# One hybrid decoder step on one Trainium2 core: a convolution, three output splits and two tail norms moved to later places, gate chunks of the layer change in other banks

## The chip, the cores and the metric

The kernel runs on one core of one Trainium2 chip. The metric is the device time of one execution in microseconds (us). A core has a matrix engine (PE, with its weight load shown apart as PEld), a vector engine (DVE), a scalar engine (ACT, which also evaluates functions from tables that it loads), GpSimd (POOL) and a queue engine (SP) that issues most transfers. Matrix products land in PSUM, which is handed out here in named banks ("tr" twice, "S" once, "y" twice, "mm" three times); everything else lives in SBUF, and DRAM is reached by DMA.

## The reference

A step takes 1024 new prompt tokens and 8 sequences of 8 sample tokens (64), through two layers and a last norm, all in float32:

```python
def rmsnorm(x, g):
    xf = x.astype(jnp.float32)
    return xf * lax.rsqrt(jnp.mean(xf * xf, axis=-1, keepdims=True) + EPS) * g.astype(jnp.float32)
...
    for i in range(DEPTH):
        mod = sc @ ada_w[i].astype(jnp.float32) + ada_b[i].astype(jnp.float32)
        shift, scale, gate = jnp.split(mod, 3, axis=-1)
        hn = (rmsnorm(x, norm_g[i]) * (1.0 + scale[:, None]) + shift[:, None]).astype(x.dtype)
...
        x = (x.astype(jnp.float32) + (1.0 + gate[:, None]) * out.astype(jnp.float32)).astype(x.dtype)
    y = rmsnorm(x, final_norm_g).astype(x.dtype)
```

Layer 0 is a Mamba-2 branch: one projection gives z, x, B, C and dt; x, B and C pass a causal convolution of width 4 and a SiLU; a chunked scan over 8 groups of heads gives y; y times SiLU(z) is normed in each group and goes through an output projection. Layer 1 is a pooling branch: a projection gives u and a gate z, u is averaged over windows of 2, 4, 8 and 16 tokens, mixed inside four groups, multiplied by SiLU(z) and projected back. The outputs are y and the new states.

## The kernel before

Activations lie transposed: a tile holds 128 channels by 1088 tokens (1024 prompt, 64 sample). A product of float32 tiles is made of three matrix products of rounded parts: `split` gives hi (ACT, a copy to a rounded type) and lo (DVE, the difference), and `mm1` (lines 188 to 192) issues hi by hi, hi by lo, lo by hi; in the trace they are lines 190, 191 and 192. Weights are streamed: a DMA brings a raw tile "wr", ACT makes "wh" (line 141), DVE makes "wl" (line 145). Tokens are taken in three chunks `CH` of 368, 368 and 352 columns.

Each engine works through its own list in order. A recording layer makes the five lists: it orders the instructions of the program by itself, and `tc.issue_after(x)` puts what stands under it behind instruction x. A tile of a pool waits until the last reader of its bank or slot is done.

**The scan with projections beside it.** While the groups are scanned (`scan_group`), PE also computes the projections of later groups (`proj_group`) and then parts of the output projection. A chunk pair of a scan runs `front` (PE transposes into a "tr" bank, ACT copies Bt out of it at line 584 and makes the decay M at lines 588 and 589, DVE makes cb at line 591, M at 594 and xd at 596), `states` (PE, line 619, S from xd and Bt) and `rows` (PE into two "y" banks, lines 641 and 645, which `evac_y` adds to x on DVE, line 611). The sample tokens end a group (`back_sample`: PE line 674 into a "y" bank, then line 611 again for 64 columns; two POOL multiplications at line 678), then come the gate (`gate`: DVE line 744, ACT square line 745), the sum of the two squares (`zsum`, line 787) and the norm (line 759 and behind). A projection tile is evicted by ACT (line 436) into "raw"; with the last chunk `proj_end` runs `conv_tile`: ACT scales, DVE adds three shifted copies (line 367, 1112 columns each), ACT takes a tanh, DVE multiplies (lines 369 and 371). For the last projected group, 6, tile ii=3 is special: it runs all three chunks at once (lines 404 to 425) and its convolution is kept for later.

**Output splits.** The rows that a group leaves go to DRAM (`gyd`). For the output projection `op_part_load` fetches them in four parts of four (`op_stage`, "gr"), and `op_split` makes gh (ACT, line 800) and gl (DVE, line 801). Parts 1 and 2 are fetched and split while later groups are scanned.

**The layer change.** `ssd_out` ends layer 0. `last_part` computes the last output tiles by chunk; for each, `sq_add` squares on ACT and adds on DVE (line 859) into "ss". `done(c)` then makes the norm of chunk c (PE line 302, ACT logarithm line 305 and exponential line 318) and `modulate` gives hn as hi and lo: for each of 8 channel tiles k, DVE multiplies (line 325), ACT adds the shift in place (line 327), ACT rounds (line 328), DVE subtracts (line 329). The other form of `modulate`, used in layer 0, makes hi straight from ACT (line 331) and lo in one DVE operation (line 332). Then `plain_pairs` computes two pairs of u and gate tiles by plain products. For each chunk c two u tiles run side by side; ACT evicts them (lines 907 and 909). Behind chunk 1 stand the gate chunks 0 and 1 of tile 0, behind chunk 2 its chunk 2, then the three gate chunks of tile 1. ACT evicts a gate chunk with a SiLU (line 940). In the trace all these product tiles are "pl". Their banks come from `plain_tile(c)`: "y" for even c, "mm" for odd c. Beside this, `act_sums` (lines 994, 997 and 998) forms the sums of activations, and `w_sums` (POOL, lines 1035, 1036 and 1040) those of weights, for the fast products (lines 1070 to 1072) that follow.

**The tail.** The last output product (`pool_layer`, loops at the end) runs over two quarters c and four tiles d, 24 matrix products each ("op", lines 1289 to 1291), evicted by DVE (line 1274). The second half of the tokens was finished before, so its squares and its two quarter norms (`norm`: PE line 302, ACT lines 305, 1782 and 318; `scale`: DVE line 1795, POOL line 1793, stores from SP) stand behind the evictions of tiles d=0, 1, 2 of the first quarter:

```python
                        if d == 0:
                            square(7, HALF, HALF)
                        elif d < 3:
                            b = HALF + QUART * (d - 1)
                            p = norm(b, QUART)
```

## Time and profile before

| | |
|---|---|
| median of 3 runs | 1591.16 us (1591.13 to 1593.46) |
| the profiled execution | 1591.15 us |
| its span, first to last instruction | 1589.0 us |
| mean granted PE clock | 0.999 |
| busy: PE, PEld | 1568.2 us (99%), 1505.1 us (95%) |
| busy: DVE, ACT, POOL | 1301.7 us (82%), 790.1 us (50%), 525.5 us (33%) |
| chain that ended last: PE, DVE, DMA, ACT | 85%, 6%, 3%, 2% |

Times of single instructions are given as microseconds from the start of the span. In a row of the timeline the first two columns are start and duration, then engine, line, operation, result<-operands with their size, how many such instructions the row joins ("x4"), and in brackets how long the engine had been idle and what released it. The duration of a row counts from when the engine took the instruction, so it can hold a wait inside the engine.

### The profile page before, as it was taken

The page shows a single profiled execution, that of the slowest core. Times are in us where ns is not written, and L with a number is a line of the kernel's source. Part 1 is how long each engine was busy: PE and PEld are TensorE (multiplying, and loading weights), DVE is VectorE, ACT ScalarE, POOL GpSimd, SP SyncE. Part 2 cuts the span into 40 slices and gives each one's busy share as a digit, 9 for nine tenths or more (in the row PEclk, how much of TensorE's full clock was granted, in tenths as well). Part 3 has the DMA queues.
Part 4 walks back from the last instruction along what each step waited for, and adds up shares of the span by engine and source line. Part 5 has one row for each costly group of instructions (what it writes and reads, how often), then busy time and mean ns, then how long its engine had stood idle before and what let it go on. Part 6 is the DMA issues. An engine that isn't in the chain of part 4 may idle for free.

```text
span 1589.0 us, 30720 instructions
## 1 busy us (share of the span) xinstructions
PE 1568.2 (99%) x11946; PEld 1505.1 (95%) x11946; DVE 1301.7 (82%) x2152; ACT 790.1 (50%) x1512; POOL 525.5 (33%) x558
## 2 busy tenths in 40 slices
PE   9999999999999999999999999999999999999997
PEld 7899999999999999989999999999999999999997
DVE  6874889887899989889888858988889777667886
ACT  6663344466766666665456348433333233233373
POOL 0133456522331413141211232366666530000241
PEclk9999999999999999999999999999999999999999
DMA  9422232365555565679999432232333379565783
GB/s 356 167 101 101 80 112 84 111 194 173 161 179 165 162 209 167 212 259 297 311 332 320 164 127 69 85 121 100 117 115 115 104 250 365 140 180 178 163 172 117
DMA packets 122304, 275.57 MB, mean 173 GB/s; under 512 B 18192, under 2 KB 59312, under 8 KB 122160
## 3 DMA queue, kind: packets, MB, share of 16 engines
q1 hardware_dynamic: 118128, 260.90, 48.4%
q0 software_dynamic: 4032, 12.72, 4.7%
q8 instruction: 94, 1.54, 0.4%
q14 instruction: 50, 0.41, 0.1%
HBM read 201.12 MB, written 70.23 MB: 171 GB/s over the span
## 4 chain that ended last, share of the span: by engine, by line
PE 85%; DVE 6%; issue 3%; DMA 3%; ACT 2%; POOL 1%; SPq 0%; DVEq 0%; ACTq 0%; POOLq 0%
PE st L1070 11%; PE st L1072 11%; PE st L1071 11%; PE mm L190 10%; PE mm L191 10%; PE mm L192 10%; PE op L1289 2%; PE op L1291 2%; PE op L1290 2%; PE y L641 2%; PE S L619 2%; PE y L645 1%; PE am L261 1%; PE tr L580 1%; PE tr L577 1%
## 5 line engine op out<-in xcount | busy, mean ns | idle before, releaser
L1072 PE MATMUL st<-hh,w 128*128 128x272 f32 x832 | 240.2, 289 | 0.0
L1070 PE MATMUL st<-hh,w 128*128 128x272 f32 x832 | 240.0, 288 | 0.0
L1071 PE MATMUL st<-hl,w 128*128 128x272 f32 x832 | 240.0, 288 | 0.0
L1070 PE MATMUL st<-t,w 128*128 128x272 f32 x624 | 179.6, 288 | 0.0
L1072 PE MATMUL st<-t,w 128*128 128x272 f32 x624 | 179.5, 288 | 0.0
L1071 PE MATMUL st<-t,w 128*128 128x272 f32 x624 | 179.2, 287 | 0.0
L190 PE MATMUL mm<-hh,wh 128*128 128x368 f32 (+1 forms) x528 | 178.9, 339 | 0.0
L191 PE MATMUL mm<-hl,wh 128*128 128x368 f32 (+1 forms) x528 | 174.0, 330 | 0.0
L192 PE MATMUL mm<-hh,wl 128*128 128x368 f32 (+1 forms) x528 | 173.2, 328 | 0.0
L1070 PEld LDWEIGHTS st<-hh,w 128*128 128x128 f32 x832 | 156.7, 188 | 0.0
L1071 PEld LDWEIGHTS st<-hl,w 128*128 128x128 f32 x832 | 156.7, 188 | 0.0
L1072 PEld LDWEIGHTS st<-hh,w 128*128 128x128 f32 x832 | 156.5, 188 | 0.0
L182 ACT ACTIVATE w<-wr 128x512 fp32r<-128x512 f32 x104 | 64.9, 629 | 165.5 <-PE st L1072 134.2
L627 POOL TENSOR_TENSOR hd<-h,cd 128x256 f32<-128x256 f32 x56 | 46.1, 824 | 285.9 <-DVE h L628 135.6
L1289 PE MATMUL op<-b,w 128*128 128x272 f32 x448 | 129.4, 289 | 0.0
L1290 PE MATMUL op<-b,w 128*128 128x272 f32 x448 | 128.8, 287 | 0.2 <-DVE b L1218 0.2
L1291 PE MATMUL op<-b,w 128*128 128x272 f32 x448 | 128.9, 288 | 0.0
L190 PE MATMUL mm<-gh,wh 128*128 128x368 f32 (+1 forms) x372 | 125.3, 338 | 0.0
L192 PE MATMUL mm<-gh,wl 128*128 128x368 f32 (+1 forms) x372 | 122.4, 329 | 0.0
L191 PE MATMUL mm<-gl,wh 128*128 128x368 f32 (+1 forms) x372 | 122.2, 328 | 0.1
L1070 PEld LDWEIGHTS st<-t,w 128*128 128x128 f32 x624 | 117.6, 189 | 0.1
L1072 PEld LDWEIGHTS st<-t,w 128*128 128x128 f32 x624 | 117.3, 188 | 0.0
(310 smaller groups left out, 4596.9 us busy)
## 6 DMA issues: line engine op xcount, KB each, us to landing
wr<-win SPq DMA_DIRECT2D x48, 512.0 KB, 3.8
wr<-pin SPq DMA_DIRECT2D x32, 512.0 KB, 3.8
acb<-acd SPq DMA_DIRECT2D x60, 256.0 KB, 4.4
wr<-pout SPq DMA_DIRECT2D x28, 512.0 KB, 5.2
x<-x1d SPq DMA_DIRECT2D x24, 544.0 KB, 6.7
x1d<-x SPq DMA_DIRECT2D x22, 544.0 KB, 6.2
wr<-pout POOLq DMA_DIRECT2D x20, 512.0 KB, 6.0
x<-xT SPq DMA_DIRECT2D x16, 544.0 KB, 6.7
```

Of the source, the lines that this page charges most:

```text
L182: self.last_hi = self.nc.scalar.activation(hi, src, AF.Copy)
L190: nc.tensor.matmul(ps[:, :n], hi[:, k, :], ah[:, a:a + n], start=first, stop=False)
L191: nc.tensor.matmul(ps[:, :n], hi[:, k, :], al[:, a:a + n], start=False, stop=False)
L192: nc.tensor.matmul(ps[:, :n], lo[:, k, :], ah[:, a:a + n], start=False, stop=last)
L619: nc.tensor.matmul(S[:, 256 * i:256 * i + 256], Bt, xde.rearrange("p r q -> p (r q)"), start=True, stop=True)
L627: nc.gpsimd.tensor_tensor(out=hd, in0=h[-1], in1=cd.unsqueeze(2).to_broadcast([P, 4, 64]), op=ALU.mult)
L1070: nc.tensor.matmul(ps[c][:, :QUART], hi[:, k], xh[:, t], start=(k == 0), stop=False)
L1071: nc.tensor.matmul(ps[c][:, :QUART], hi[:, k], xl[:, t], start=False, stop=False)
L1072: nc.tensor.matmul(ps[c][:, :QUART], lo[:, k], xh[:, t], start=False, stop=(k == 3))
L1289: nc.tensor.matmul(ps[:, :QUART], hi[:, k], xh, start=k == 0, stop=False)
L1290: nc.tensor.matmul(ps[:, :QUART], hi[:, k], xl, start=False, stop=False)
L1291: nc.tensor.matmul(ps[:, :QUART], lo[:, k], xh, start=False, stop=k == 7)
```

## The change

It has four parts, and the work that is computed is the same.

1. In group 6, the convolution of projection tile ii=2 is called at the start of tile ii=3 instead of with the last eviction of ii=2, and its first DVE addition (line 367) is put behind the eviction of the last rows of the prompt (`row_evict`, line 611).
2. `op_split` of parts 1 and 2 puts the ACT copy gh behind the last copy Bt recorded so far (`front_copy`, line 584).
3. Layer change: gate chunk 0 of tile 0 goes to a "tr" bank, gate chunks 1 and 2 of tile 0 to "mm" banks. In layer 1, k=0 of `modulate` uses the direct form (lines 331 and 332 of before). The evictions of u chunk 0 stand behind the first rounding of chunk 1 (`mod_first[1]`). The additions of squares of chunk 2 stand behind the exponential of chunk 1's norm (`root`).
4. Tail: the two quarter norms of the second half stand behind tiles d=2 and d=3 instead of d=1 and d=2.

```diff
@@ -317,3 +317,3 @@
     def rstd(self, rst):
-        self.nc.scalar.activation(rst, rst, AF.Exp, scale=-0.5)
+        return self.nc.scalar.activation(rst, rst, AF.Exp, scale=-0.5)
 
@@ -325,3 +325,3 @@
         nc.vector.scalar_tensor_tensor(out=t[:, :pn], in0=x[:, a:a + pn], scalar=self.scl[l][:, k, 8:9], in1=rst[:, a:a + pn], op0=ALU.mult, op1=ALU.mult)
-        if l:
+        if l and k:
             nc.scalar.activation(t[:, :pn], t[:, :pn], AF.Identity, bias=sh)
@@ -330,3 +330,3 @@
         else:
-            nc.scalar.activation(hi[:, a:a + pn], t[:, :pn], AF.Identity, bias=sh)
+            self.mod_hi = nc.scalar.activation(hi[:, a:a + pn], t[:, :pn], AF.Identity, bias=sh).ins
             last = nc.vector.scalar_tensor_tensor(out=lo[:, a:a + pn], in0=t[:, :pn], scalar=sh, in1=hi[:, a:a + pn].bitcast(F32), op0=ALU.add, op1=ALU.subtract)
@@ -366,3 +366,4 @@
         for k in range(1, 4):
-            nc.vector.scalar_tensor_tensor(out=acc[:, :n], in0=raw[:, k:k + n], scalar=w[k], in1=acc[:, :n], op0=ALU.mult, op1=ALU.add)
+            with self.tc.issue_after(self.row_evict) if k == 1 and ti == 2 * BESIDE[-1] else contextlib.nullcontext():
+                nc.vector.scalar_tensor_tensor(out=acc[:, :n], in0=raw[:, k:k + n], scalar=w[k], in1=acc[:, :n], op0=ALU.mult, op1=ALU.add)
         nc.scalar.activation(raw[:, :n], acc[:, :n], AF.Tanh)
@@ -397,2 +398,3 @@
 
+        raws = []
         for ii in range(4):
@@ -400,4 +402,5 @@
             raw = self.proj_begin(G, ii)
+            raws.append(raw)
             if (G["g"], ii) == (BESIDE[-1], 3):
-
+                self.proj_end(G, 2, raws[2], True)
                 ps = [self.mm_tile() for _ in CH]
@@ -427,3 +430,3 @@
                 self.mm3(ps, w, self.hn, CH[c])
-                self.proj_evict(G, ii, raw, ps, c)
+                self.proj_evict(G, ii, raw, ps, c, (G["g"], ii) != (BESIDE[-1], 2))
                 if c != (0, 0, 2, 0)[ii]:
@@ -583,3 +586,3 @@
                 Bt = gp.tile([P, 128], F32, tag="Bt", bufs=2, name=self.name("Bt"))
-                nc.scalar.activation(Bt, pt[:, 256:384], AF.Copy)
+                self.front_copy = nc.scalar.activation(Bt, pt[:, 256:384], AF.Copy).ins
             M = gp.tile([P, 4, 128], F32, tag="M", bufs=3, name=self.name("M"))
@@ -610,4 +613,4 @@
             y = xs[q]
-            nc.vector.scalar_tensor_tensor(out=y[:, tok], in0=y[:, tok], scalar=self.vec[:, V_D + 2 * g + q:V_D + 2 * g + q + 1], in1=py[:, :L],
-                                           op0=ALU.mult, op1=ALU.add)
+            return nc.vector.scalar_tensor_tensor(out=y[:, tok], in0=y[:, tok], scalar=self.vec[:, V_D + 2 * g + q:V_D + 2 * g + q + 1],
+                                                  in1=py[:, :L], op0=ALU.mult, op1=ALU.add).ins
 
@@ -646,3 +649,3 @@
             for q in range(2):
-                evac_y(py[q], q, slice(128 * c, 128 * c + 256), 256)
+                self.row_evict = evac_y(py[q], q, slice(128 * c, 128 * c + 256), 256)
 
@@ -797,5 +800,6 @@
 
-    def op_split(self, raw):
+    def op_split(self, raw, part):
         hi, lo = self.slots.get("gh", F32R, short=True), self.slots.get("gl", F32R, short=True)
-        self.nc.scalar.activation(hi, raw, AF.Copy)
+        with self.tc.issue_after(self.front_copy) if 0 < part < 3 else contextlib.nullcontext():
+            self.nc.scalar.activation(hi, raw, AF.Copy)
         self.nc.vector.tensor_tensor(out=lo, in0=raw, in1=hi.bitcast(F32), op=ALU.subtract)
@@ -810,6 +814,6 @@
             if st is not None:
-                out.append(self.op_split(st))
+                out.append(self.op_split(st, part))
             st = nx
             yield
-        out.append(self.op_split(st))
+        out.append(self.op_split(st, part))
         yield
@@ -886,3 +890,4 @@
                 else:
-                    self.sq_add(ss, x[d], d, False, a, n, nc.vector)
+                    with self.tc.issue_after(self.root) if l == 0 and c == 2 else contextlib.nullcontext():
+                        self.sq_add(ss, x[d], d, False, a, n, nc.vector)
                 if c == 2 and d % 2 and nt == 4:
@@ -953,3 +958,3 @@
         def z_tile(p, w, c, ch):
-            ps = self.plain_tile(c)
+            ps = self.pp.tile([P, 512], F32, tag="tr", bufs=2, name=self.name("pl")) if p == c == 0 else self.plain_tile(1 if p == 0 else c)
             self.mm3(ps, w, self.hn, ch)
@@ -963,4 +968,5 @@
                     self.mm1(ps[i], ws[i], k, self.hn[k], ch, k == 0, k == 7)
-            for i in range(2):
-                self.u_chunk(U[i], ps[i], ch)
+            with self.tc.issue_after(self.mod_first[1]) if c == 0 else contextlib.nullcontext():
+                for i in range(2):
+                    self.u_chunk(U[i], ps[i], ch)
             if c == 1:
@@ -1686,3 +1692,3 @@
         ss, rst = sl.get("ss"), sl.get("rst")
-        self.hn = []
+        self.hn, self.mod_first = [], []
 
@@ -1695,5 +1701,7 @@
                 self.ms_log(ss, rst, a, n, 1.0 / 1024)
-                self.rstd(rst[:, a:a + n])
+                self.root = self.rstd(rst[:, a:a + n]).ins
             for k in range(8):
                 self.modulate(1, k, x[k], rst, self.hn[k][0], self.hn[k][1], a, n, x[k][:, a:a + n])
+                if k == 0:
+                    self.mod_first.append(self.mod_hi)
 
@@ -1823,4 +1831,4 @@
                             square(7, HALF, HALF)
-                        elif d < 3:
-                            b = HALF + QUART * (d - 1)
+                        elif d > 1:
+                            b = HALF + QUART * (d - 2)
                             p = norm(b, QUART)
```

Where the lists differ, at three places. DVE around the end of group 4's samples, before; "raw" is the accumulator of the convolution (line 367), "xbc_122" and "xbc_123" the two row tiles, "y" the banks that are evicted (line 611 in before, 614 in after), "gl" an output split, and line 744 (747 in after) the gate:

```order
L611 SCALAR_TENSOR_TENSOR xbc_122_7412<-xbc_122_7412,vec_193,y1133_8312 128x256
L367 SCALAR_TENSOR_TENSOR raw1130_8291<-raw1102_8102,cwh_270,raw1130_8291 128x1112
L611 SCALAR_TENSOR_TENSOR xbc_123_7600<-xbc_123_7600,vec_193,y1134_8313 128x256
L367 SCALAR_TENSOR_TENSOR raw1130_8291<-raw1102_8102,cwh_270,raw1130_8291 128x1112
L611 SCALAR_TENSOR_TENSOR xbc_122_7412<-xbc_122_7412,vec_193,y1143_8376 128x64
L367 SCALAR_TENSOR_TENSOR raw1130_8291<-raw1102_8102,cwh_270,raw1130_8291 128x1112
L611 SCALAR_TENSOR_TENSOR xbc_123_7600<-xbc_123_7600,vec_193,y1144_8380 128x64
L801 TENSOR_TENSOR gl_139_8404<-gr_132_8364,gh_138_8403 128x1088
L369 SCALAR_TENSOR_TENSOR xbc_131_8288<-raw1102_8102,raw1130_8291 128x1024
L371 SCALAR_TENSOR_TENSOR xbc_131_8288<-raw1102_8102,raw1130_8291 128x64
L801 TENSOR_TENSOR gl_142_8419<-gr_137_8401,gh_141_8418 128x1088
L744 TENSOR_TENSOR xbc_122_7412<-xbc_122_7412,z_129_8230 128x1088
```

and after:

```order
L614 SCALAR_TENSOR_TENSOR xbc_122_7412<-xbc_122_7412,vec_193,y1132_8301 128x256
L614 SCALAR_TENSOR_TENSOR xbc_123_7600<-xbc_123_7600,vec_193,y1133_8302 128x256
L368 SCALAR_TENSOR_TENSOR raw1139_8335<-raw1102_8102,cwh_270,raw1139_8335 128x1112 x2
L614 SCALAR_TENSOR_TENSOR xbc_122_7412<-xbc_122_7412,vec_193,y1143_8376 128x64
L368 SCALAR_TENSOR_TENSOR raw1139_8335<-raw1102_8102,cwh_270,raw1139_8335 128x1112
L614 SCALAR_TENSOR_TENSOR xbc_123_7600<-xbc_123_7600,vec_193,y1144_8380 128x64
L805 TENSOR_TENSOR gl_139_8404<-gr_132_8364,gh_138_8403 128x1088
L747 TENSOR_TENSOR xbc_122_7412<-xbc_122_7412,z_129_8230 128x1088
L370 SCALAR_TENSOR_TENSOR xbc_131_8332<-raw1102_8102,raw1139_8335 128x1024
L372 SCALAR_TENSOR_TENSOR xbc_131_8332<-raw1102_8102,raw1139_8335 128x64
L805 TENSOR_TENSOR gl_142_8419<-gr_137_8401,gh_141_8418 128x1088
```

Both evictions of 256 columns now stand in front of the three additions, and the first gate multiplication has moved from behind the second output split to behind the first.

ACT in the scan that runs with output part 2, before; "M" is the decay of a front (lines 588 and 589), "Bt" the copy out of the "tr" bank (line 584), "gh_184" an output split (line 800):

```order
L141 ACTIVATE wh1353_9598<-wr1315_9406 128x1024
L800 ACTIVATE gh_184_9850<-gr_181_9747 128x1088
L588 ACTIVATE M1363_9645<-acb1329_9488,tka1_1448 128x128 x3
L584 ACTIVATE Bt1362_9643<-tr1361_9638 128x128
L588 ACTIVATE M1363_9645<-acb1329_9488,tka1_1448 128x128
L569 ACTIVATE ea1376_9707<-acb1343_9553 128x512
L589 ACTIVATE M1363_9645<-M1363_9645 128x512
```

and after, where these lines are 591, 592, 587 and 804:

```order
L591 ACTIVATE M1391_9794<-acb1359_9634,tka1_1448 128x128
L572 ACTIVATE ea1388_9785<-acb1359_9634 128x512
L591 ACTIVATE M1391_9794<-acb1359_9634,tka1_1448 128x128 x3
L572 ACTIVATE ea1407_9867<-acb1375_9705 128x512
L587 ACTIVATE Bt1390_9792<-tr1389_9787 128x128
L592 ACTIVATE M1391_9794<-M1391_9794 128x512
L804 ACTIVATE gh_184_9850<-gr_181_9747 128x1088
L141 ACTIVATE wh1397_9828<-wr1355_9602 128x1024
L591 ACTIVATE M1410_9876<-acb1375_9705,tka0_1447 128x128 x4
L576 ACTIVATE es1434_10021<-acb1406_9865 128x32
L592 ACTIVATE M1410_9876<-M1410_9876 128x512
```

The copy gh_184 has left the place in front of M1363 and Bt1362 and stands behind the two fronts that follow: M1391 and Bt1390 are now in front of it.

PE at the end of u chunk 2 in the layer change, before; "pl1705" and "pl1706" are the two u tiles of chunk 2, "pl1707" the gate chunk 2 of tile 0, "pl1711" the gate chunk 1 of tile 1, whose weights are wh1696 and wl1697:

```order
L190 MATMUL pl1706_11926<-hh_243_11510,ws1688_11739 128x352
L191 MATMUL pl1706_11926<-hl_244_11511,ws1688_11739 128x352
L192 MATMUL pl1706_11926<-hh_243_11510,ws1689_11740 128x352
L190 MATMUL pl1711_12062<-hh_229_11496,wh1696_11761 128x368
L191 MATMUL pl1711_12062<-hl_230_11497,wh1696_11761 128x368
L190 MATMUL pl1707_11979<-hh_229_11496,wh1691_11745 128x352
L191 MATMUL pl1707_11979<-hl_230_11497,wh1691_11745 128x352
```

and after:

```order
L190 MATMUL pl1706_11926<-hh_243_11510,ws1688_11739 128x352
L191 MATMUL pl1706_11926<-hl_244_11511,ws1688_11739 128x352
L192 MATMUL pl1706_11926<-hh_243_11510,ws1689_11740 128x352
L190 MATMUL pl1707_11979<-hh_229_11496,wh1691_11745 128x352
L191 MATMUL pl1707_11979<-hl_230_11497,wh1691_11745 128x352
L192 MATMUL pl1707_11979<-hh_229_11496,wl1692_11746 128x352
```

The two products of pl1711 that stood in front of pl1707 have gone to their own tile, which follows pl1710, the gate chunk 0 of tile 1.

## Prediction

> **What bounds the kernel now.** I read the page first: how busy each engine is, and then which waits PE has.
>
> ```profile
> span 1589.0 us, 30720 instructions
> PE 1568.2 (99%) x11946; PEld 1505.1 (95%) x11946; DVE 1301.7 (82%) x2152; ACT 790.1 (50%) x1512; POOL 525.5 (33%) x558
> ```
>
> PE stands still for 1589.0 - 1568.2 = 20.8 us of the span, and the matrix work itself is not changed. So the change can gain only from those 20.8 us. The view of PE's waits, all of them by releaser, shows which part of it lies where the change works (total us, times, longest):
>
> ```profile
> PE pl L190 <- ACT pz L940: 2.5, 1, 2.5
> PE y L674 <- DVE xbc L611: 1.4, 1, 1.4
> PE S L619 <- DVE xd L596: 1.1, 1, 1.1
> ...
> PE ms L302 <- DVE ss L1776: 1.0, 1, 1.0
> ...
> PE mm L825 <- ACT gh L800: 0.7, 1, 0.7
> ...
> PE mm L825 <- ACT raw L436: 0.4, 1, 0.4
> PE pl L190 <- ACT u L907: 0.3, 1, 0.3
> ```
>
> Each part of the change meets some of these: the convolution the y, raw and gh waits (2.5 together), the splits the S wait (1.1), the layer change the two pl waits and a third of 0.51 that a row below shows (3.3), the tail the ms wait (1.0). If all went and nothing came back the gain would be 7.9 us. For each I then read the timeline of the engines around it to see what is late next.
>
> **The convolution (about 690 to 708 us): nothing.** The timelines of DVE, POOL and PE, in this order:
>
> ```profile
> 689.59 0.47 DVE L611 SCALAR_TENSOR_TENSOR xbc<-xbc,vec,y 128x256 f32<-128x256 f32 x1
> 689.98 2.66 DVE L367 SCALAR_TENSOR_TENSOR raw<-raw,cwh,raw 128x1112 f32<-128x1112 f32 x1
> 692.56 0.47 DVE L611 SCALAR_TENSOR_TENSOR xbc<-xbc,vec,y 128x256 f32<-128x256 f32 x1
> 695.72 1.36 DVE L367 SCALAR_TENSOR_TENSOR raw<-raw,cwh,raw 128x1112 f32<-128x1112 f32 x1
> 704.47 1.28 DVE L744 TENSOR_TENSOR xbc<-xbc,z 128x1088 f32<-128x1088 f32 x1
> 688.54 5.89 POOL L678 TENSOR_TENSOR h<-h,es 128x1024 f32<-128x1024 f32 x2
> 693.08 0.34 PE L674 MATMUL y<-M,zsc 128*64 128x64 f32 x4 [1.42 <-DVE xbc L611]
> 707.94 0.43 PE L825 MATMUL mm<-gh,wh 128*128 128x368 f32 x1 [0.71 <-ACT gh L800]
> ```
>
> PE waits at 693.08 for a "y" bank, since the second eviction stood on DVE behind a convolution addition of 2.66 us. The same addition takes 1.36 at 695.72, when POOL is done: beside POOL's two multiplications it waits some 1.3 us for one of them, and the evictions, which read PSUM, do not (0.47 beside POOL). After the change the second eviction runs at about 690 and the wait of 1.42 goes. But DVE has no idle time between 689.59 and 704.47, it has the same instructions to do, and the second gate multiplication at 704.47 keeps its place behind all of them. ACT's square of it and, behind that, the copy gh release PE at 707.94. PE gets there 1.42 us earlier and waits 1.42 longer. What would be earned at 693 comes back at 708. I take 0, between -1.4 (DVE's list gets shorter by as much) and +0.3 (the evictions of group 6's tile shift behind it).
>
> **The splits (802 us): -1.1.** ACT, DVE and PE:
>
> ```profile
> 799.04 1.11 ACT L800 ACTIVATE gh<-gr 128x1088 fp32r<-128x1088 f32 x1 [5.30 <-DMA gr<-gyd]
> 811.94 0.26 ACT L584 ACTIVATE Bt<-tr 128x128 f32<-128x128 f32 x1
> 801.22 0.29 DVE L591 TENSOR_TENSOR cb<-tr,kc 128x128 f32<-128x128 f32 x1 [4.68 <-ACT Bt L584]
> 802.26 0.67 PE L619 MATMUL S<-xd,Bt 128*128 128x256 f32 x2 [1.13 <-DVE xd L596]
> 816.41 1.28 DVE L801 TENSOR_TENSOR gl<-gr,gh 128x1088 fp32r<-128x1088 f32 x1
> 836.52 0.60 DVE L842 SCALAR_TENSOR_TENSOR x<-mm,gat,x 128x368 f32<-128x368 f32 x1 [1.73 <-PE mm L192]
> ```
>
> ACT stood 5.30 us at the copy gh for its DMA, and the front's decay, Bt, cb and xd stood behind it. Now gh stands behind the Bt of the second later front (811.94), and they do not wait for it. Queued behind it there are one weight part and the next decay, which it holds for its own 1.11 us and no longer, since its DMA has long landed. Its difference on DVE keeps its place (816.41), so gh, made by about 814 (Bt, the end of that decay and its own 1.11), has some 2 us to spare. Behind the gain DVE waits for PE (1.73 at 836.52), so PE leads and keeps it. -1.1, between 0 and -1.13.
>
> **The layer change (990 to 1006 us): +0.2.** PE, POOL and DVE, with one weight difference without POOL beside it (706.87) to compare:
>
> ```profile
> 993.99 0.43 PE L190 MATMUL pl<-hh,ws 128*128 128x352 f32 x1 [2.46 <-ACT pz L940]
> 1001.20 0.43 PE L190 MATMUL pl<-hh,wh 128*128 128x368 f32 x1 [0.51 <-ACT wh L141]
> 1006.05 0.33 PE L192 MATMUL pl<-hh,wl 128*128 128x368 f32 x1
> 1000.62 1.67 POOL L1035 TENSOR_TENSOR sw<-wr 128x512 f32<-128x512 f32 x1 [10.80 <-PE pl L191]
> 706.87 1.22 DVE L145 TENSOR_TENSOR wl<-wr,wh 128x1024 fp32r<-128x1024 f32 x1
> 1001.18 2.19 DVE L145 TENSOR_TENSOR wl<-wr,wh 128x1024 fp32r<-128x1024 f32 x1
> 1003.30 1.80 DVE L994 TENSOR_TENSOR x<-x 128x544 f32<-128x544 f32 x1
> 1005.02 1.81 DVE L998 TENSOR_TENSOR t<-x,t 128x544 fp32r<-128x544 f32 x1
> 1006.76 0.71 DVE L994 TENSOR_TENSOR x<-x 128x544 f32<-128x544 f32 x1
> ```
>
> The second u tile of chunk 2 waits 2.46 us for the SiLU of gate chunk 0, which held its "y" bank. With that chunk in "tr" and the other two in "mm" this goes, and so do the wait of 0.3 for a u eviction before it (the last line of the waits) and, as placed, the 0.51 behind: 3.27 us. PE would then come 3.27 us earlier to pl1710. Two products of pl1711 now come later; from 1001.20 to 1006.05 lie 28 products (2 of pl1711, 24 of pl1707, 2 of pl1710), 0.173 us each, so they are 0.35 us of work that is still to do. -3.27 + 0.35 = -2.9 is the lower bound.
>
> But the end of u chunk 2 is also what releases POOL's weight sums: the one at 1000.62 waited for PE, and now starts 2.46 + 0.3 earlier, at about 997.9; two more of its operations follow (lines 1036 and 1040). POOL and DVE take turns here: beside POOL three DVE operations took 2.19 - 1.22 = 0.97, 1.80 - 0.71 = 1.09 and 1.81 - 0.71 = 1.10 longer. Before, only the first of these three fell on or ahead of wl1697 (1001.18 to 1003.37), the weight part that PE's third product of pl1710 reads at 1006.05. After, POOL's three operations meet five DVE operations that all stand ahead of wl1697 (four of line 994, one of 998), so all three delays do: 1003.37 + 1.09 + 1.10 = 1005.56. The squares of chunk 2, put later, push chunk 2's modulation and all DVE behind it by some 0.35 more (an estimate: two additions of 0.5 us that now come among the modulation): 1005.9. So PE takes that product at 1005.9 instead of 1006.05, with 0.35 us more work behind it: +0.2. The 3.27 us are waited for at pl1710. With a fourth delay of 1.1 it is +1.3, the upper bound. Behind that DVE is where it was, since the three delays have only moved.
>
> The three stretched rows alone do not say that a meeting must cost that much; an overlap in part would leave the sum anywhere down to -2.9. [...]
>
> **The tail (1559 us): -1.0.** DVE, PE:
>
> ```profile
> 1558.22 1.35 DVE L1776 TENSOR_TENSOR ss<-ss,sq 128x544 f32<-128x544 f32 x2
> 1559.00 0.73 PE L302 MATMUL ms<-ss,ones 128*128 128x272 f32 x2 [1.04 <-DVE ss L1776]
> 1562.58 0.62 PE L302 MATMUL ms<-ss,ones 128*128 128x272 f32 x2
> 1561.80 2.13 DVE L1795 SCALAR_TENSOR_TENSOR y<-x,vec,ms 128x272 f32<-128x272 f32 x5
> 1578.65 0.50 DVE L1274 SCALAR_TENSOR_TENSOR x<-op,gat,x 128x272 f32<-128x272 f32 x1 [1.90 <-PE op L1291]
> ```
>
> The first norm product now comes one tile later, 1562.58 - 1559.00 = 3.58 us by the rows of the two norms. The sum that it reads is ready by 1558.22 + 1.35 = 1559.57, so the wait of 1.04 goes. The scalings of both norms (2.13 us each on DVE), POOL's and the stores on SP shift with it; DVE still waits 1.90 us for PE at the last eviction, which covers a part pushed that far. Without that cover the last eviction would slip by what is over. PE leads from here to its last product, so the end moves with it. -1.0, between -1.04 and +0.3.
>
> **Sum.** 0 - 1.1 + 0.2 - 1.0 = -1.9 on the profiled 1591.15: 1589.25, say 1589.3. The median (1591.16) stands 0.01 from the profiled execution. About 0.2% (3.2 us) is what a measurement of this kernel can tell from no change, so -1.9 counts as the same.
>
> **Rivals.** *The delays do not meet in the layer change* (chance 0.22): POOL starts late enough, or PE has enough else to do, and the gain there is the full 2.9. Then 1591.15 - 1.1 - 1.0 - 2.9 = 1586.1. For it: nothing in the order forces POOL to run at once. Against: it is released by the very product that comes earlier.
>
> *The convolution's wait stays away* (0.07): DVE saves at 704.47 what the evictions gained, 1.42 more: 1587.9. Against: DVE has no gap there to give up.
>
> *The splits and the tail give back what they gain* (0.11): another wait, of the front's own transfer or of an eviction, ends at the same time: 1591.15 + 0.2 = 1591.4. For it: the S wait had a predecessor chain of four instructions, any of which can be late for its own reason.
>
> *Slower: chunk 2's norm comes too late* (0.05). Its squares now stand behind the exponential of chunk 1. If that puts them behind the whole modulation of chunk 1 on DVE, the norm and chunk 2's modulation slip by about 8 x (0.55 + 0.45) = 8 us, from these rows:
>
> ```profile
> 974.15 1.11 DVE L325 SCALAR_TENSOR_TENSOR x<-x,scl,rst 128x368 f32<-128x368 f32 x2
> 994.58 0.21 DVE L342 TENSOR_TENSOR hl<-x,hh 128x64 fp32r<-128x64 f32 x1
> 992.80 0.45 DVE L329 TENSOR_TENSOR hl<-x,hh 128x288 fp32r<-128x288 f32 x1
> ```
>
> The last part of chunk 2's hn is made at 994.8. PE finished u chunk 2 at 1001.20 - 0.51 = 1000.7 and would now finish at 997.9, so it wants that part for its last six products, at 996.9. So 2.1 us are free; a slip beyond 2.1 + 1.9 = 4.0 us makes the kernel slower than before, and 8 us give 1589.25 + 5.9 = 1595.1. Against: only one of the two additions has moved in DVE's order, by 14 places, and the last one stands where it was.
>
> **How the numbers follow.** Forecast 0.55 and the four rivals 0.22, 0.07, 0.11, 0.05. The range reaches below to the first rival and half a microsecond on, and above to the third and half a microsecond on, which takes in a part of the layer change's upper bound: 1585.6 to 1591.9. Faster by over 0.2% (below 1588.0) is the first rival, most of the second, and the edge of the forecast: 0.30. Slower by over 0.2% (above 1594.3) is most of the last: 0.04. The rest, 0.66, is the same.
>
> **What would show it.** Right: no PE wait at the y products near 692 us, but one of about 2 us at the first gh product near 707; no wait at S near 801; no wait for pz, but some 4 us of waits at the first three products of pl1710 for wh and wl, with POOL's line 1035 starting near 996.8 (the earlier gain counted) and DVE's rows beside it stretched by 1.1 each; no wait at the ms product near 1560. Wrong: wl1697 ready before 1003, or a PE wait in the scan after 840 that was not there, or ms products of chunk 2 over 2 us late.

## The result, and the profile after

The changed kernel takes 1598.76 us (median of 6 runs, 1596.80 to 1599.96); the kernel before, in as many runs beside it, 1591.14 (1589.57 to 1593.46). The ratio is 1.0046 [1.0033, 1.0059]: 7.3 us slower by the ratio, outside the range, and on the side to which the prediction gave 0.04. The profiled execution took 1599.07, with a span of 1596.9, so it stands for the median.

The page's head of the changed kernel, and its waits of PE (total us, times, longest). Lines have shifted: 994, 997 and 998 are now 1000, 1003 and 1004; POOL's sums 1035, 1036 and 1040 are 1041, 1042 and 1046; 1070 to 1072 are 1076 to 1078.

```profile
span 1596.9 us, 30719 instructions
PE 1572.6 (98%) x11946; PEld 1508.2 (94%) x11946; DVE 1299.6 (81%) x2152; ACT 790.9 (50%) x1512; POOL 530.3 (33%) x558
```

```profile
PE st L1076 <- ACT w L182: 7.6, 1, 7.6
PE mm L829 <- ACT gh L804: 2.0, 1, 2.0
...
PE pl L192 <- DVE wl L145: 0.3, 1, 0.3
...
PE pl L190 <- ACT u L914: 0.2, 1, 0.2
```

The waits that the change aimed at (pz 2.5, y 1.4, S 1.1, ms at the tail 1.0) have all gone from the list. In their place stand one wait of 7.6 us that no part of the prediction names and, as forecast, one of 2.0 at the first gh product. PE is also busy 1572.6 - 1568.2 = 4.4 us longer with as many instructions, which means that some of them ran slower.

Counted by products (the nth of one profile against the nth of the other), PE stands 1.5 us earlier than before at the gh product of 703.72, 1.1 later at 781.87, 0.2 earlier at the S product (802.26) and 0.3 earlier behind it, 2.5 earlier from 1010 to 1023, 5.3 later at the first T product (1023.28), 9.1 later from 1026.5 on, and 7.9 later at the end, behind the tail. So the convolution cost 1.1 instead of nothing, 1.4 were earned at the S product that the splits aim at, the layer change cost 9.4, and the tail earned 1.2. Nearly all of the surprise lies between 998 and 1036 us.

POOL there, in the changed kernel (start, duration, operation, and in brackets the idle time before it with its releaser):

```profile
998.17 13.69 POOL L1041 TENSOR_TENSOR sw<-wr 128x512 f32<-128x512 f32 x1 [7.55 <-PE pl L191]
1011.94 1.30 POOL L1042 TENSOR_TENSOR sw<-sw,wr 128x512 f32<-128x512 f32 x1
...
1014.56 0.29 POOL L922 COPY npl<-u 128x120 f32<-128x120 f32 x1
```

The first sum, released at 998.17 as the prediction said (about 997.9), is in execution for 13.69 us. Its sister behind it takes 1.30. DVE in the same stretch:

```profile
998.69 2.62 DVE L1000 TENSOR_TENSOR x<-x,x 128x544 f32<-128x544 f32 x4
1001.23 0.71 DVE L1004 TENSOR_TENSOR t<-x,t 128x544 fp32r<-128x544 f32 x1
1001.87 1.21 DVE L145 TENSOR_TENSOR wl<-wr,wh 128x1024 fp32r<-128x1024 f32 x1
1003.00 0.71 DVE L1000 TENSOR_TENSOR x<-x 128x544 f32<-128x544 f32 x1
...
1009.29 1.42 DVE L928 TENSOR_TENSOR ws<-u 128x1222 f32<-128x1222 f32 x1
1022.32 0.73 DVE L1004 TENSOR_TENSOR t<-x,t 128x544 fp32r<-128x544 f32 x1 [11.61 <-ACT t L1003]
```

No row of DVE is stretched: line 1000 takes 0.71, line 145 takes 1.21, as without POOL. DVE has no gap until 1009.29 + 1.42 = 1010.71, and POOL's sum ends at 998.17 + 13.69 = 1011.86, 1.15 later. The two engines did not take turns. DVE kept the turn, and POOL got in when DVE's list broke off.

What hung on POOL is seen on SP's queue and on ACT, in the changed kernel:

```profile
1014.88 0.34 SPq L923 DMA_DIRECT2D npT<-npl  x1
...
1015.78 13.48 SPq L948 DMA_DIRECT2D zgd<-pz  x2
```

```profile
1021.64 0.66 ACT L1003 ACTIVATE t<-x 128x544 fp32r<-128x544 f32 x1 [14.05 <-DMA zgd<-pz]
...
1027.95 0.61 ACT L182 ACTIVATE w<-sw 128x512 fp32r<-128x512 f32 x1
```

and in before:

```profile
1007.64 0.34 SPq L918 DMA_DIRECT2D npT<-npl  x1
...
1009.06 12.29 SPq L943 DMA_DIRECT2D zgd<-pz  x2
```

```profile
1014.28 0.66 ACT L997 ACTIVATE t<-x 128x544 fp32r<-128x544 f32 x1 [3.89 <-DMA zgd<-pz]
```

POOL's two copies into npl end 7.2 us later (1014.85 against 1007.62), and so their store (line 923) comes 7.2 later. SP took its list in order: behind that store stand a weight load and the two gate stores zgd, issued from 1015.78 instead of 1009.06. A T operand of ACT takes the slot that the first gate store frees: 1021.64 instead of 1014.28, 7.36 later. The weight part w of line 182 is behind it on ACT, and PE waits for it.

PE and its granted clock there, in the changed kernel (the columns of the windows are us, PE busy with the instructions begun, granted clock, DMA share, GB/s):

```profile
1028.62 0.60 PE L1076 MATMUL st<-t,w 128*128 128x272 f32 x1 [7.63 <-ACT w L182]
...
1030.52 0.43 PE L1076 MATMUL st<-t,w 128*128 128x272 f32 x1
1030.74 0.43 PE L1077 MATMUL st<-t,w 128*128 128x272 f32 x1
```

```profile
1024.00:1028.00 4.00, 0.00 (x0) 0.67 0.00 0
1028.00:1032.00 4.00, 2.70 (x10) 0.50 0.35 139
1032.00:1036.00 4.00, 4.00 (x21) 0.55 0.41 131
1036.00:1040.00 4.00, 4.00 (x34) 1.00 0.66 251
```

After the wait of 7.63 us the clock is about half for 6.9 us, until 1035.5: a product every 0.23 us, 21 in a window of 4 us instead of 34. With a second wait of 0.68 us (at 1030.12, for the other part of the weight, from DVE's line 184) this makes the other 3.8 us (5.3 to 9.1), of which some 3.1 are the slow clock, the largest part of the 4.4 us by which PE is busier.

### The profile page after: what moved, and what is told of

Its sections match the earlier page's. It is cut to its first block, busy times and chain, and to the rows that moved or that the text cites. A ratio compares the mean times of both kernels' runs of the same rounds, so it can differ in the third digit from the quotient of the medians.

```text
span 1596.9 us, 30719 instructions
## 1 busy us (share of the span) xinstructions
PE 1572.6 (98%) x11946; PEld 1508.2 (94%) x11946; DVE 1299.6 (81%) x2152; ACT 790.9 (50%) x1512; POOL 530.3 (33%) x558
## 4 chain that ended last, share of the span: by engine, by line
PE 88%; DVE 6%; DMA 3%; ACT 1%; POOL 1%; issue 1%; SPq 0%; DVEq 0%; ACTq 0%; POOLq 0%
PE st L1078 11%; PE st L1076 11%; PE st L1077 11%; PE mm L190 11%; PE mm L191 11%; PE mm L192 11%; PE op L1296 2%; PE op L1297 2%; PE op L1295 2%; PE y L644 2%; PE S L622 2%; PE y L648 1%; PE am L261 1%; PE tr L583 1%; PE tr L580 1%
```

## The experiments

The theory from these rows (**starvation**, theory A of the expectations): POOL's sum reads SBUF as DVE's additions and subtractions do, and while DVE's next operation is ready when one ends, the sum is held (its row took 13.69 us in the changed kernel). In before DVE had a gap of 0.03 us just then; the change closed it. All else (npl, SP's queue, the T slot, w, the clock) follows. The "port" in three of the expectations is the author's name for what the two engines contend for: the rows show how long POOL is held, and no run shows by what. The rivals: **the queue alone** (the banks or the moved evictions delay the store in some other way, and POOL's 13.69 is only POOL waiting with everyone), and **a sum of small losses** (convolution, splits and tail cost time which the long wait merely collects). Each kernel was timed beside the kernel before on the same chip; the ratio is to that.

**The changed kernel with the old banks.**

```
-            ps = self.pp.tile([P, 512], F32, tag="tr", ...) if p == c == 0 else self.plain_tile(1 if p == 0 else c)
+            ps = self.plain_tile(c)
```

> The changed kernel with the banks of the gate chunks put back (tile 0's chunk 0 and 2 in y, as before); all else of the change stays. Theory A, early POOL: with the banks the end of u chunk 2 comes 2.5 to 3 us earlier, POOL's first weight sum is released into a stretch in which DVE goes from one two-input operation to the next without a gap, and does not get the shared port for 13.7 us; all that stands behind it (two sums, two copies, the store npT, and on SP's queue behind that the stores of the gate) comes late, and PE waits 7.6 us for a weight part and then runs some 7 us at about half clock. With the old banks the 2.46 us wait for the gate chunk is back, line 1041 starts near 1000 and runs within 2 us, and the 7.6 us wait is gone: 1591.15 + 1.1 (convolution) - 1.3 (splits) - 1.2 (tail) = 1589.8. Theory B, the other edits of the layer change (direct k=0, evictions and squares behind) make it slow by the order that they give DVE: the 7.6 us wait stays, 1597 to 1599.

1592.43 (12 runs), ratio 1.0009 [0.9997, 1.0022], so the banks carry most of the loss. But ten runs lie between 1590.2 and 1593.8 and two at 1598.2 and 1601.05. The profiled one is the longest, and shows the same thing there as the changed kernel, with the pz wait back (theory A had expected the long wait to be gone):

```profile
1002.90 12.17 POOL L1041 TENSOR_TENSOR sw<-wr 128x512 f32<-128x512 f32 x1 [10.41 <-PE pl L191]
```

```profile
PE st L1076 <- ACT w L182: 6.4, 1, 6.4
PE pl L190 <- ACT pz L945: 2.6, 1, 2.6
```

So the banks are not what holds POOL. With them, by the times, it came in every run of the changed kernel and of the next one; without them, in this kernel, in two of twelve. That speaks for a race between POOL and DVE's list and against the queue alone.

**The banks alone**, on before (the same line, nothing else).

> The kernel before with the banks of the gate chunks alone changed. Theory A: PE's wait of 2.46 us goes, POOL is released at about 998, and if DVE has no gap there it is held 10 us or more and PE waits some 7 us at the first product that needs the late weight: 1598 to 1600. Theory B: the banks are not the cause; the wait of 2.46 goes and little comes back, 1588.7 to 1591.

1598.97 (5 runs), 1.0048 [1.0036, 1.0060]: the whole loss, without any other edit. That is the end of the sum of small losses.

```profile
998.07 13.28 POOL L1035 TENSOR_TENSOR sw<-wr 128x512 f32<-128x512 f32 x1 [8.60 <-PE pl L191]
```

**The changed kernel with gaps in DVE's list**: behind each of the 16 subtractions of line 1000 a memset of one column, which reads nothing.

```
-            nc.vector.tensor_tensor(out=out, in0=x, in1=y, op=ALU.subtract)
+            ins = nc.vector.tensor_tensor(out=out, in0=x, in1=y, op=ALU.subtract)
+            with self.tc.issue_after(ins.ins):
+                nc.vector.memset(gap, 0.0)
```

> The changed kernel with a DVE memset of one column behind each of the 16 subtractions of activations in the layer change (DVE operations that read nothing from SBUF). Theory A: POOL's waiting sum gets the port at the first of them, line 1041's row falls from 13.69 to under 3 us, POOL's three sums end by about 1004, the 7.6 us wait goes; DVE loses about 1.1 us to each sum and some 1.6 us to the memsets, so pl1710 waits 2 to 4 us instead: 1587.5 to 1590. If instead POOL's sum is slow by itself (or waits for its data), its row stays at 13 us and the time at 1598 or above.

1593.93 (11 runs), 1.0011 [1.0002, 1.0020]: some 5 us of the loss come back by giving DVE more to do. The time expected was lower. POOL and DVE in it:

```profile
999.83 1.78 POOL L1044 TENSOR_TENSOR sw<-wr 128x512 f32<-128x512 f32 x1 [7.57 <-PE pl L191]
1001.69 1.65 POOL L1045 TENSOR_TENSOR sw<-sw,wr 128x512 f32<-128x512 f32 x1
```

```profile
1000.39 1.81 DVE L1001 TENSOR_TENSOR x<-x,x 128x544 f32<-128x544 f32 x1
1000.41 0.06 DVE L1003 MEMSET gap<- 128x1 f32 x1
```

The memset ends at 1000.47, and POOL's sum ends 1.14 us later, at 1001.61: it went in at that gap. From there the two do take turns, DVE's operations are stretched by 1.1 (1.81 instead of 0.71), and PE waits at pl1710 nearly as the prediction had it (first for a u eviction, not for wh):

```profile
PE pl L190 <- ACT u L914: 2.4, 1, 2.4
...
PE pl L192 <- DVE wl L145: 1.2, 1, 1.2
```

3.6 us of waits there, against "some 4" in the prediction. What was missed here too is the clock behind them: 0.91 from 990 to 1010 and 0.84 from 1010 to 1020, where before has 1.00.

**The changed kernel with the npT store behind the gate stores.** If the harm comes through SP's order, POOL may starve as long as it likes once nothing urgent stands behind its store.

```
-        nc.sync.dma_start(self.io["npT"][p], npl)
+        with self.tc.issue_after(self.z_last) if p == 0 else contextlib.nullcontext():
+            nc.sync.dma_start(self.io["npT"][p], npl)
...
-        self.nc.sync.dma_start(self.zgd[p], dst)
+        ins = self.nc.sync.dma_start(self.zgd[p], dst).ins
+        if p == 1:
+            self.z_last = ins
```

> The changed kernel with the store npT of u tile 0 put behind the two gate stores of tiles 0 and 1 on SP's queue. Theory A with its chain by way of SP: POOL's sum is still held for some 13 us, but the gate store of tile 0 is issued near 1006 instead of 1015.8, ACT's split t that takes its slot starts near 1012 to 1014 instead of 1021.6, and PE's wait of 7.6 us shrinks below 1: 1587 to 1589. If the late weight sums themselves make PE wait (by way of POOL's sums, not of SP's stores), the wait stays at 5 us or more: 1596 to 1598.

1589.49 (11 runs), 0.9981 [0.9973, 0.9990]: 9 us under the changed kernel, and faster than before. POOL's sum, and the gate stores on SP, which now don't wait for it (the npT store is issued at 1026.11):

```profile
999.78 20.75 POOL L1044 TENSOR_TENSOR sw<-wr 128x512 f32<-128x512 f32 x1 [7.56 <-PE pl L191]
```

```profile
1006.19 17.08 SPq L949 DMA_DIRECT2D zgd<-pz  x2
```

POOL is held even longer, 20.75 us, and it costs nothing: PE has no wait above 0.6 us in this stretch. So the two links are apart: the starvation is the cause, SP's order is what makes it cost.

**The same store on before**, as a control.

> The kernel before with the store npT of u tile 0 put behind the two gate stores, as in the fourth run. A control: PE does not wait for what hangs on these stores in the kernel before, so 0, 1591.5. If the store's place earns by itself, 1588 to 1590.

1591.46 (11 runs), 0.9999 [0.9990, 1.0008]. The store's place alone is worth nothing where POOL isn't starved.

**One more operation on DVE, on before.** If the gap decides, one more two-input operation ahead of wl1697 must close it, with the banks, the evictions and the store as they were. (The operation writes a tile that nobody reads.)

```
+            self.nsub += 1
+            if self.nsub == 5:
+                with self.tc.issue_after(ins.ins):
+                    t = self.gp2.tile([P, HALF], F32, tag="mt2", ...)
+                    nc.vector.tensor_tensor(out=t, in0=out, in1=out, op=ALU.add)
```

> The kernel before, nothing of the change, with one more DVE operation of 0.64 us (two SBUF inputs, its result unused) ahead of the weight difference wl1697. Theory A: in the kernel before POOL's first sum gets the port in a gap of some 0.03 us, in which DVE waits for wh1696 (1001.15 to 1001.18). With DVE 0.64 us later and ACT's wh ready first, that gap closes; the sum is held for some 10 us and PE waits 5 to 8 us, then runs at half clock for some us: 1598 to 1601, for 0.64 us of DVE work. Rival: POOL is held only by single operations, as I had assumed in the prediction; then +0 to +0.7, 1591.5 to 1592.2.

1599.47 (7 runs), 1.0039 [1.0025, 1.0054]; six of the seven between 1597.7 and 1602.5, one at 1592.4. The 0.64 us of an operation that nothing needs cost 7.4 by the medians (6.2 [4.0, 8.6] by the ratio):

```profile
1000.26 12.41 POOL L1041 TENSOR_TENSOR sw<-wr 128x512 f32<-128x512 f32 x1 [10.80 <-PE pl L191]
```

```profile
998.17 0.72 DVE L1000 TENSOR_TENSOR more<-x 128x544 f32<-128x544 f32 x1
...
1000.71 0.72 DVE L1004 TENSOR_TENSOR t<-x,t 128x544 fp32r<-128x544 f32 x1
1001.35 1.22 DVE L145 TENSOR_TENSOR wl<-wr,wh 128x1024 fp32r<-128x1024 f32 x1
```

```profile
PE st L1076 <- ACT w L182: 5.3, 1, 5.3
PE pl L190 <- ACT pz L940: 2.4, 1, 2.4
```

The pz wait is still there, POOL is released at the usual time, and the long wait has come all the same. What differs from before is that line 145 follows without a gap.

**The parts.** The convolution alone, on before (its three edits of the diff):

> The kernel before with the part on the convolution alone. Theory: one wait of 2.0 us at the gh product near 707 in place of 1.4, 0.35 and 0.7, and PE at about half clock for the 3.5 us behind it: slower by 1.1, 1592.5. Rival: 0 (1591.5) or -1.4 (1590.1), with PE at full clock behind the wait.

1592.82 (11 runs), 1.0010 [1.0001, 1.0019]: a small loss, about as expected. PE waits 1.98 us at the gh product (708.34). The window behind it, of this kernel:

```profile
708.00:712.00 4.00, 3.66 (x10) 0.57 0.96 347
```

against before

```profile
708.00:712.00 4.00, 3.86 (x22) 1.00 0.90 297
```

The three small waits have become one of 1.98 us, and behind it the clock is down to 0.57: 10 instructions begin in 4 us instead of 22. The size of the loss isn't settled. Between 685 and 750 us, counted by products against before, PE loses 1.0 to 2.6 us in all five profiles of kernels with this part. Of the seven kernels without it, besides before, five lose nothing there, and two lose 0.9 and 1.7, with y waits of 2.1 and 2.5 in place of 1.4. And the kernel with the gaps loses 1.8 there at a clock of 1.00, with waits of 0.6 at a y product and 1.0 at an S product ahead of the gh product: the clock is not all of the cost.

The splits and the tail, on before (their edits of the diff):

> The kernel before with the splits and the tail alone (the two parts that the prediction put at -1.1 and -1.0). Theory: both waits are gone and nothing comes back, 1591.5 - 2.2 = 1589.3. Rival: POOL's release in the layer change comes 1.1 us earlier in absolute time but not against DVE, so nothing else moves; if it did, some executions would show the long wait of 7 us and lie near 1597.

1590.77 (11 runs), 0.9996 [0.9987, 1.0005]: not to be told from before by the medians. In its trace, whose execution took 1589.28, neither the S nor the ms wait of before is left. The gain lies inside the interval, -2.1 to +0.8 us.

Whether these parts took the waits away is answered by the other profiles. The ms wait of 1.0 stands in all six of kernels without the tail's part and in none of the seven with it. The S wait is different: of the six kernels without the splits' part only before has it. In the other five the transfer that ACT's gh waits for landed earlier, and PE begins S without a wait; these are the rows of the control, before with the store moved (ACT stood 3.84 us there, in before 5.30):

```profile
798.23 1.11 ACT L800 ACTIVATE gh<-gr 128x1088 fp32r<-128x1088 f32 x1 [3.84 <-DMA gr<-gyd]
```

```profile
801.19 1.02 PE L619 MATMUL S<-xd,Bt 128*128 128x256 f32 x4
```

So the S wait belonged to the one execution of before that was profiled, and no run shows that the splits' part earns anything.

**What beats both.** Three versions with the moved store: the changed kernel without the convolution, the banks and the store alone on before, and these with the splits and the tail.

> The changed kernel with the store npT of u tile 0 behind the gate stores, and without the part on the convolution (as before there). Theory: the convolution part costs about 1.1 us, since the waits near 693 and 703 go but one wait of 2.0 us at 707 takes their place and PE then runs some 3.5 us at about half clock. Without it 1589.5 - 1.1 = 1588.4. Rival: the convolution part is neutral (what I had predicted), 1589.5, or earns 1.4, then 1590.9.

> The kernel before with two edits: the banks of the gate chunks (second run) and the store npT behind the gate stores (fourth run). Theory A: POOL's first sum is still held for over 10 us, but nothing that PE needs hangs on it, so the banks earn what their waits were, 1591.5 - 2.5 = 1589.0, where the banks alone gave 1599. Rival: POOL's late sums themselves make PE wait, 1594 or more.

> The run before this one with the splits and the tail as in the changed kernel; without the convolution part and the other edits of the layer change. Theory: the sum of its parts, 1589.0 - 0.8 to 1589.0 - 2.2, so 1587 to 1588.2, the fastest of all. If the convolution part or the other edits of the layer change earn anything, it is slower than the fourth run (1589.5).

| kernel | median us (runs) | ratio to before |
|---|---|---|
| changed kernel, store moved | 1589.49 (11) | 0.9981 [0.9973, 0.9990] |
| the same without the convolution | 1588.99 (11) | 0.9983 [0.9974, 0.9992] |
| before with the banks, store moved | 1587.21 (5) | 0.9970 [0.9958, 0.9981] |
| the same with splits and tail | 1587.57 (8) | 0.9974 [0.9964, 0.9983] |

The shortest is the smallest edit: the one line of the banks and one store, 4.8 us [3.0, 6.7] under before, more than was expected. In its trace POOL is starved for 16.54 us, and nobody minds: PE has no wait above 0.7 us there.

```profile
996.83 16.54 POOL L1038 TENSOR_TENSOR sw<-wr 128x512 f32<-128x512 f32 x1 [8.59 <-PE pl L191]
```

That the starved POOL leaves DVE's operations unstretched helps here, since wl1697 is then early (line 145 took 1.21 and ended at 1001.33; in before it took 2.19 and ended at 1003.37). In this profile PE gains 2.3 us on before between 960 and 1026, most of the 2.9 that the prediction gave as the lower bound of the layer change; another 1.4 is the S wait, which these edits don't touch. The last two rows of the table differ by less than their intervals, so whether splits and tail add anything to it stays open. The first two rows don't differ either, so they don't show the cost of the convolution; in the profile of the second PE loses 1.7 in that stretch without it, behind the y wait of 2.5. Why the first two rows are some 2 us behind the last two is not shown by the medians, whose intervals overlap. What sets the second row apart from the fourth are the direct form at k=0 and the moved evictions and squares. The profiles point to them: between 960 and 1026 PE gains 2.3 us on before in each of the last two kernels and 0.9 in each of the first two. But no run has those edits alone.

## Why the prediction was wrong

**The layer change: the step that failed** is "POOL and DVE take turns here", and with it "POOL's three operations meet five DVE operations ..., so all three delays do". Up to there it held: the pz wait went, u chunk 2 ended about as much earlier as said, and POOL was released at 998.17 (forecast 997.9). Then it assumed that a POOL operation which meets DVE gets the next turn, and that each meeting costs DVE its full 1.1 us; that was the author's estimate. The three stretched rows of before (0.97 to 1.10 longer) showed that the two alternated once POOL was in; they did not show how it got in. It got in through a gap. These are the rows of before that ought to have been read for that:

```profile
1000.43 0.72 DVE L998 TENSOR_TENSOR t<-x,t 128x544 fp32r<-128x544 f32 x1
```

```profile
1000.09 1.06 ACT L141 ACTIVATE wh<-wr 128x1024 fp32r<-128x1024 f32 x1
```

Line 998 ends at 1001.15, wh1696 is ready at 1000.09 + 1.06 = 1001.15, and wl1697, which needs it, begins at 1001.18. (Rows of DVE without a gap overlap a little: line 998 begins at 1000.43, and the row ahead of it ends at 1000.51. So 0.03 us is a real stop.) POOL's sum ends at 1000.62 + 1.67 = 1002.29, so it began to work 1.15 before, at 1001.14: in that gap. In the changed kernel wh1696 is ready at 1000.72 + 1.04 = 1001.76, before DVE ends the row ahead of wl1697 (1001.23 + 0.71 = 1001.94), and there is no gap. In before wh1696 was late because PE's products at the end of u chunk 2 were. There it began 0.07 us after ACT's row ahead of it had ended, too little for a bracket; in the kernel with the convolution alone, where PE is later still, the row names what it waits for:

```profile
1002.98 1.06 ACT L141 ACTIVATE wh<-wr 128x1024 fp32r<-128x1024 f32 x1 [1.56 <-PE pl L191]
```

So in before the wait that the change removed was what let POOL in. That the gap decides is shown by the two experiments on DVE's list (memsets open one and 5 us come back; one operation more closes it and 7 are lost). That it hangs on u chunk 2 rests on these rows. It is a race with DVE's list and not a matter of PE alone: in the profile of the changed kernel with the old banks the pz wait was back, but DVE's list stood later (line 1004 ends at 1003.82, wh1696 was ready at 1003.63), and there was no gap.

The trace of before held a warning on POOL as well, which was not read. Beside another gapless stretch of DVE a copy of three columns took 6.40 us:

```profile
705.34 6.40 POOL L351 COPY ncv<-raw 128x3 f32<-128x3 f32 x1 [10.91 <-ACT raw L436]
```

The second thing missed is what stands behind POOL. The prediction priced its three sums by what they do to DVE, and never followed what waits for POOL: two copies, a store in the middle of SP's order, and behind it the gate stores. That chain is worth 7.63 us of waiting and 0.68 at a second weight part, and the clock behind it some 3.1 more. +0.2 was forecast, 9.4 came.

Of the forecast's own marks, "wl1697 ready before 1003" was set as a sign of being wrong. It was ready at 1003.08, and the product that needs it ran at 1003.14 instead of 1006.05. That is earlier than the sum allows: the mark's reason held, its number was a little too strict. The sign of being right that stayed away says it more clearly: "some 4 us of waits at the first three products of pl1710" were 0.2 and 0.3, and no row of DVE was stretched.

**The convolution: wrong by 1.1** (by the medians of it alone 1.6 [0.2, 3.0]). The y wait went and came back at the gh product, 1.98 instead of 0.71, as said ("PE gets there 1.42 us earlier and waits 1.42 longer"). The gate's second multiplication came 0.35 earlier only (704.12 against 704.47), and so did the first eviction (689.23 against 689.59): DVE's list between them is as long as before, as said. Two of the three additions still stand beside POOL's two multiplications, with 2.6 us each:

```profile
690.01 5.24 DVE L368 SCALAR_TENSOR_TENSOR raw<-raw,cwh,raw 128x1112 f32<-128x1112 f32 x2
```

What was left out is that three waits of 1.4, 0.7 and 0.4 need not be the same as one of 2.0. The window 708 to 712 of the changed kernel has the clock at 0.58, where before has 1.00:

```profile
708.00:712.00 4.00, 4.00 (x14) 0.58 0.92 335
```

The kernel with the gaps paid as much at a full clock, so the clock is what cost it here and not in every kernel.

**The splits: the number came, by luck.** The S wait is gone and 1.4 earned at that product (1.1 forecast); ACT's gh of that part has time to spare, as said. But five kernels without this part don't have the wait either. The prediction took for a property of the kernel what a late transfer did in one execution. **The tail: right.** The ms wait is gone and 1.2 earned (1.0 forecast), and the wait goes with the edit in every profile. The size comes from single profiles; the medians of these two parts alone could not show it.

**The rivals.** "The delays do not meet in the layer change" had the right mechanism (nothing forces POOL to run at once) with the wrong sign: POOL did not run, PE stood 2.5 us earlier than before until 1023, and lost 11.6 behind it. The slower rival that was given, chunk 2's norm, did not occur: the waits of PE hold nothing of it.

## What to carry to other kernels

Before a wait is removed, look at which other engine works in the hole that it leaves: here a gap of 0.03 us in DVE's list let POOL's sum in, and where it was closed the sum took 12.17 to 20.75 us. If POOL's results go out on a queue that is worked in order, as SP's was here, put nothing urgent behind them; with that done, a POOL starved for 16.54 us cost nothing and most of the removed wait was earned. Before a wait of one profile is put into a sum, see whether a second profile has it: the S wait was in one of six. And don't take a short PE wait that moves into another one as free: behind the one wait of 1.98 us the windows show a clock of 0.57 to 0.69 in four kernels.

## What was not expected of the hardware

**POOL's first sum was held for as long as DVE's list ran on, in a row of up to 20.75 us.** The end of POOL's first sum against the end of DVE's last operation before its list broke off (in the row of the gaps, of the memset; in the last row, of the last operation ahead of one of three columns):

| kernel | POOL's sum took | DVE's run ends | POOL ends | between |
|---|---|---|---|---|
| changed | 13.69 | 1010.71 | 1011.86 | 1.15 |
| old banks | 12.17 | 1013.92 | 1015.07 | 1.15 |
| banks alone | 13.28 | 1010.20 | 1011.35 | 1.15 |
| store behind | 20.75 | 1019.38 | 1020.53 | 1.15 |
| one more on DVE | 12.41 | 1011.54 | 1012.67 | 1.13 |
| gaps in DVE's list | 1.78 | 1000.47 | 1001.61 | 1.14 |
| before, banks, store moved | 16.54 | 1012.21 | 1013.37 | 1.16 |

An operation of 1.15 us thus took between 1.78 and 20.75, by nothing but DVE's list. The last row is no stop of DVE. Its next operation, of three columns, was taken at 1012.13 without a gap, and POOL went ahead of it:

```profile
1012.13 1.26 DVE L929 TENSOR_TENSOR ws<-ws,kc 128x3 f32<-128x3 f32 x1
```

POOL's second sum was then held again in that kernel, for 4.26 us (1013.45 to 1017.71), behind five operations of DVE that ran unstretched until 1016.57. And behind an operation of DVE that itself had to wait, POOL was next although DVE was ready: in before line 145 (2.19) ends at 1003.37, line 994 was taken at 1003.30, and POOL's second sum ends at 1002.37 + 2.15 = 1004.52, 1.15 after line 145. So POOL can be the one that waits, which the prediction had not considered. In these profiles POOL did not get in between two full-width DVE operations that were both ready, of which the first ran unstretched. Why it did behind a stretched one is not shown.

**The clock fell behind a wait of 2 us, in four kernels of five.** Behind the wait of 1.98 at the gh product the windows show 0.58 (changed), 0.57 (convolution alone), 0.69 (store behind) and 0.62 (old banks, 712 to 716), but 1.00 in the kernel with the gaps, whose wait there is also 2.0. The changed kernel with the store moved and without the convolution, with a y wait of 2.5, shows 0.97 over 640 to 700, where before has 1.00. Behind the pz wait of 2.5 before shows 1.00 from 990 to 1010 and the convolution alone 0.91. So what the same wait costs differs from kernel to kernel. What decides it is not shown by any run here.
